# Strassen's seven products for the strided query and key tiles of a hybrid decoder trunk

## The chip, the cores and the metric

The kernel runs on one core of a Trainium2 chip. The metric is the device time of one execution in microseconds. Engines are named as in the profile: PE (TensorE, matrix products; PEld is its weight load), DVE (VectorE), ACT (ScalarE), POOL (GpSimd, which here mostly issues DMAs) and SP (SyncE, which issues DMAs). Each engine takes its instructions in the order in which the program wrote them; an instruction that waits holds back all that stand behind it on the same engine.

## The reference

A two-layer decoder trunk on x of 512 tokens by 1024 features. Layer 0 mixes tokens with dilated window attention, layer 1 with a gated linear recurrence; each is followed by a gated FFN with a short causal convolution, and each part is wrapped in a norm before and a norm after. The change touches layer 0's attention alone:

```
WINDOWS, DILATIONS = (128, 512, 2048), (1, 4, 16)
qkv = (x @ w_qkv).reshape(B, S, N_GROUPS, 3, HEADS_PER_GROUP, HEAD_DIM)   # 3 groups of 8 heads of 128
for g in range(N_GROUPS):
    o, lse = dilated_group_attention(qkv[:, :, g, 0], qkv[:, :, g, 1], qkv[:, :, g, 2], ...)
alpha = jax.nn.softmax(jnp.stack(lses), axis=0)
o = jnp.sum(alpha[..., None] * jnp.stack(outs), axis=0)
return o.reshape(B, S, ATTN_OUT_WIDTH) @ w_o
```

Group 0 (dilation 1) is called local here, groups 1 and 2 strided. Both strided groups are computed together, with the tokens permuted by their residue mod 4.

## The kernel before

**Split weights.** Every large product is done in three passes over float32r parts: both operands are split into a high part (a rounded copy, made by ScalarE, line 144) and a low part (the difference, made by VectorE, line 145), and high x high, high x low, low x high are summed in PSUM (`mm3`, L325). So a tile of 128 features by 512 tokens over 1024 rows is 8 x 3 = 24 matmuls of 512 columns.

**The supply of weights.** `plan` lists all weight chunks in order, one raw chunk of 1 MB each, loaded by SP (`load`, L267) into three raw buffers. `refill` turns a chunk into pieces, in order; `pump` takes the next piece, if one of the 16 weight buffers (`HALVES`, counted in `state["live"]`) is free, and splits it. `take` hands a piece to the matmuls, `done` gives its buffers back. `tick` is called after each tile: it lets the side tasks go on (`side`: softmax work written as generators, which yield how many ticks to wait) and then pumps one or two pieces.

**The attention, as it stands.** Per pair of heads (`hp`), four pairs. The local stage computes values, queries and keys of group 0 with 24-matmul tiles, with `local` as a side task for each head. Then come four strided rounds, each of eight query and key tiles (`feat_tiles(4, ...)`, L325, for two groups), four value blocks of 24 matmuls (`values`, L1028), and two heads as side tasks (`strided`). A head multiplies queries and keys (S, L1124), adds the bias and takes the maximum (VectorE), exponentiates (ScalarE), normalises, transposes in VectorE, stores the result to DRAM (`turned`, L368), fetches it back transposed (`fetched`, eight DMAs, L375) and broadcasts a row of factors (`cn`, L1160); all these DMAs are issued by POOL. Some ticks later it multiplies by the values (O, L1179). The value blocks go through DRAM to be permuted (SP, L1040 and L1053). `qk` (L941, L943) scales a finished tile out of PSUM, permuting it. After the rounds, `rows_run` multiplies by `w_o` and applies the norms.

**Strassen in the FFN.** `seven` already does this for eight chunks of the FFN's upward product. A chunk of 1024 rows by 256 features is seen as 2 x 2 blocks, and so is the token operand: four products of one block of features, rows and tokens for each half of the result, eight in all, become seven products of sums of blocks, each 4 x 3 matmuls of 256 columns (L830). The token side's sums are made once per layer (`token_sums`): 8 passes to add the parts, 8 to combine, 8 splits. They take the buffer of x (`x_sb`), which is saved to DRAM and fetched back by `x_back`, and one or two gain buffers. The weight side's sums are made in the raw chunk, some by VectorE (L195, L199), some by a DMA issued on POOL that adds a block from DRAM into the raw tile (`add_rows`, L181). `slot` emits one product or one filling quarter, then what `later` put off, then a tick.

**Order.** The program order is fixed by hand; there is no scheduler that moves instructions.

Of the kernel before, what the change touches and what calls it, by code (L numbers as in the profile page):

```python
# [11 lines left out]
F32 = mybir.dt.float32  # L12
# [6 lines left out]
P = 128  # L19
# [21 lines left out]
CYCLE = 15  # L41
HALF = ("s1", "w11", "w12", "a22", "s2", "s3", "s4")
# [36 lines left out]
def kernel(  # L79
# [136 lines left out]

    def refill():

        i = state["cv"]
        if i >= state["dma"]:  # L220
            return
# [13 lines left out]
    def pump(limit=2):  # L235

        for _ in range(limit):
# [4 lines left out]
            if pieces and state["live"] + 2 - (pieces[0][0][1] in HALF) <= HALVES:  # L242
# [47 lines left out]
    def tick():  # L290
        for s in list(sides):
            s[0] -= 1
# [436 lines left out]
    def token_sums(hT, T):  # L729

        assert len(sides) == 1
        d = dp.tile([P, 4, D], F32, name=nm("x_kept"))
        nc.gpsimd.dma_start(d, X[0])
        kept.append(d)
        homes = cp.tile([P, 4, D], F32R, tag="x_sb", name=nm("T"))
        homes = [homes[:, n] for n in range(4)]
        homes += [cp.tile([P, D], F32R, tag="gain", name=nm("T"), bufs=2) for _ in range(2)]
        homes = [[h[:, 0:512], h[:, 512:1024]] for h in homes]
        homes += [[gen(F32R, "T") for _ in range(2)] for _ in range(2)]
# [9 lines left out]
        tt = nc.vector.tensor_tensor  # L749

# [14 lines left out]
        for k in range(2):  # L765
            tt(b12[k], b12[k], b22[k], op=ALU.subtract)
            tt(b22[k], b22[k], b11[k], op=ALU.add)
# [3 lines left out]
        yield 8  # L771
        parted(2, b12)
        yield 3
        b21 = whole(4, 0)
        yield 1
        for k in range(2):
            tt(b21[k], b21[k], b22[k], op=ALU.subtract)
# [5 lines left out]
    def seven(hT, T, begin, before):  # L783

        due = []

        def later(n, f):
            due.append([n, f])

        def slot(emit):  # L790
            emit()
            for d in list(due):
                d[0] -= 1
                if d[0] < 0:
                    due.remove(d)
                    d[1]()
            tick()
# [7 lines left out]
        right = {  # L805
            1: block(0, 0), 2: block(1, 0), 3: block(1, 1), 5: turn(0), 6: turn(1), 7: turn(2), 4: turn(3),
        }

# [45 lines left out]
        def quarters(i, m, j, b):  # L854
            ps = []

            def quarter(n):
                W = take(i, m)
                if not n:
                    ps.append(psum())  # L860
                for k in (2 * n, 2 * n + 1):
                    mm3(
                        ps[0], [w[k // 4][:, k % 4, :] for w in W], [h[:, k, :] for h in hT], k == 0, k == KD - 1
                    )
                if n % 2:
                    done(1)
                if n == 3:
                    later(1, lambda: finish(b, ps[0], j))

            return [lambda n=n: quarter(n) for n in range(4)]  # L870

        steps = {}
        fill = quarters(before, 1, SEVEN[0] - 1, 3)
        for n, j in enumerate(SEVEN):
# [3 lines left out]
            steps.update((CYCLE * n + m, q) for m, q in zip((1, 2, 6, 7, 10, 11, 12, 13), fill + quarters(i, 0, j, 2)))  # L878
            fill = quarters(i, 1, j, 3)
# [4 lines left out]
        fill += quarters(after, 0, SEVEN[-1] + 1, 0)  # L884
# [10 lines left out]
    def attention(hT, post, pre):  # L895
# [119 lines left out]
        def values(vs, permute, midway=None):  # L1015

            if permute:
                vd = dp.tile([S, 512], F32, name=f"vrows{len(vrows)}")
                vrows.append(vd)
            ids = [chunk(), chunk()]  # L1020
            banks = {}
            for t in range(4):
                banks[t] = psum("v")
                for u in range(4):
                    W = take(ids[u // 2], u % 2)
                    steps = [(k, a, b) for k in (2 * u, 2 * u + 1) for a, b in PASSES]
                    for k, a, b in steps:
                        mm(  # L1028
                            banks[t],
# [404 lines left out]
```

## Time and profile before

| | |
|---|---|
| median of 3 runs | 1443.12 us (1443.1 to 1443.16) |
| profiled execution | 1443.5 us |
| its span | 1441.7 us |
| busy PE / DVE / ACT / POOL | 1433.2 / 924.9 / 674.7 / 179.5 us |
| granted TensorE clock | 0.999 |

The profile's page gives busy times of each engine, a picture of the span in 40 slices, DMA queues, the chain of work that ended last, and the costliest groups of instructions. A row of a group names the line, engine, operation, out<-in tiles, shapes and count, then total busy time and mean nanoseconds of one, then the idle time before them and what ended it. A row of the timeline has the start, the length, the engine, line, operation and, in brackets, the idle time before it with the engine or DMA that ended it. A row of the stage windows has start:end, then the length, then busy time (and number of instructions) of PE, PEld, DVE, ACT and POOL, the granted clock, the share of the DMA engines and GB/s. Busy times count an instruction from its start to its end; back to back they overlap a little.

### The profile page before, as it was taken

What the parts mean: (1) busy time and instruction counts of PE and PEld (TensorE: products, weight loads), DVE (VectorE), ACT (ScalarE), POOL (GpSimd) and SP (SyncE); (2) the same over time, 40 slices, a digit from 0 to 9 for tenths busy, and PEclk for the clock granted to TensorE, in tenths of its full rate; (3) what the DMA queues carried; (4) which work ended last, traced back from release to release, by engine and by line L of the source; (5) the groups of instructions that cost most, each with busy time, mean ns of one, the idle gap of its engine ahead of it and who ended that gap; (6) DMA issues with size and microseconds to landing.
All of it is one profiled execution on the core that took longest, in us unless ns stands there. A gap on an engine that the chain in (4) does not pass through costs nothing.

```text
span 1441.7 us, 20040 instructions
## 1 busy us (share of the span) xinstructions
PE 1433.2 (99%) x7437; PEld 1229.6 (85%) x7437; DVE 924.9 (64%) x1851; ACT 674.7 (47%) x1380; POOL 179.5 (12%) x311
## 2 busy tenths in 40 slices
PE   9999999999999999999999999999999999999998
PEld 7888888888888898989988888888898899988886
DVE  6555635353536889877774348869789977774333
ACT  7333424141415555555543335589455555553331
POOL 0441514040402101101000001000100111000000
PEclk9999999999999999999999999999999999999999
DMA  7653546364636345554452322431435645453201
GB/s 224 206 150 108 170 119 187 127 182 132 182 133 191 117 147 122 145 133 104 142 205 88 108 82 88 132 117 59 146 98 155 150 107 128 126 189 117 88 0 59
DMA packets 142842, 189.63 MB, mean 132 GB/s; under 512 B 9312, under 2 KB 119352, under 8 KB 142232
## 3 DMA queue, kind: packets, MB, share of 16 engines
q1 hardware_dynamic: 114280, 145.48, 31.6%
q0 software_dynamic: 27616, 41.82, 12.4%
q8 instruction: 58, 0.95, 0.3%
q10 hardware_dynamic: 848, 1.05, 0.2%
q14 instruction: 40, 0.33, 0.1%
HBM read 168.83 MB, written 19.49 MB: 131 GB/s over the span
## 4 chain that ended last, share of the span: by engine, by line
PE 92%; ACT 4%; DVE 3%; issue 0%; DMA 0%; DVEq 0%; ACTq 0%
PE ps L325 44%; PE acc L325 24%; PE ps L830 11%; PE v L1028 8%; PE v L956 1%; DVE xb L1237 1%; PE O L1179 1%; PE S L1124 1%; PE S L1078 1%; DVE wlo L145 1%; ACT sig L1258 1%; ACT whi L144 1%; PE O L325 1%; PE tr L407 1%; ACT sig L1277 0%
## 5 line engine op out<-in xcount | busy, mean ns | idle before, releaser
L325 PE MATMUL ps<-hT,whi 128*128 128x512 f32 (+1 forms) x2240 | 644.9, 373 | 0.0
L144 ACT ACTIVATE whi<-raw 128x512 fp32r<-128x512 f32 x552 | 326.1, 626 | 322.6 <-PE ps L325 122.2
L145 DVE TENSOR_TENSOR wlo<-raw,whi 128x512 fp32r<-128x512 f32 x552 | 360.8, 686 | 180.1 <-ACT whi L144 180.1
L325 PEld LDWEIGHTS ps<-hT,whi 128*128 128x128 f32 x2240 | 403.9, 189 | 68.4
L325 PE MATMUL ps<-hT,wlo 128*128 128x512 f32 (+1 forms) x1120 | 415.7, 371 | 0.0
L325 PEld LDWEIGHTS ps<-hT,wlo 128*128 128x128 f32 x1120 | 211.0, 188 | 37.2
L325 PE MATMUL acc<-whi,ahi 128*128 128x512 f32 x512 | 199.6, 390 | 0.0
L325 PE MATMUL acc<-whi,alo 128*128 128x512 f32 x512 | 199.3, 389 | 0.1
L325 PE MATMUL acc<-wlo,ahi 128*128 128x512 f32 x512 | 199.2, 389 | 0.0
L678 DVE SCALAR_TENSOR_TENSOR u<-ps,cols,u 128x511 f32<-128x511 f32 x192 | 143.7, 748 | 48.9 <-ACT u L674 45.5
L325 PEld LDWEIGHTS acc<-whi,alo 128*128 128x128 f32 x512 | 96.1, 188 | 20.5 <-DVE alo L145 0.5
L325 PEld LDWEIGHTS acc<-wlo,ahi 128*128 128x128 f32 x512 | 96.1, 188 | 19.8
L325 PEld LDWEIGHTS acc<-whi,ahi 128*128 128x128 f32 x512 | 96.1, 188 | 19.7
L674 ACT ACTIVATE u<-ps,cols 128x512 f32<-128x512 f32 x96 | 74.0, 770 | 82.3 <-DVE ps L845 41.9
L1028 PE MATMUL v<-whi,hT 128*128 128x512 f32 x320 | 102.3, 393 | 0.0
L830 PE MATMUL ps<-T,whi 128*128 128x256 f32 x512 | 92.8, 280 | 0.0
L181 POOL DMA_DIRECT2D raw<-in_ffn_w_up_dram x32 | 41.5, 1475 | 362.0 <-DVE wlo L145 207.8
L368 POOL DMA_DIRECT2D turned<-T x36 | 19.6, 547 | 523.7 <-DVE T L362 522.4
L375 POOL DMA_DIRECT2D ft<-turned x144 | 78.8, 555 | 43.4 <-issue 18.1
L830 PEld LDWEIGHTS ps<-T,whi 128*128 128x128 f32 x512 | 80.1, 189 | 1.6
L830 PE MATMUL ps<-T,wlo 128*128 128x256 f32 x256 | 71.8, 280 | 0.0
L1028 PEld LDWEIGHTS v<-whi,hT 128*128 128x128 f32 x320 | 60.1, 188 | 12.2
(194 smaller groups left out, 1483.9 us busy)
## 6 DMA issues: line engine op xcount, KB each, us to landing
raw<-in_ffn_w_up_dram SPq DMA_DIRECT2D x48, 1024.0 KB
raw<-in_attn_w_qkv_dram SPq DMA_DIRECT2D x67, 512.0 KB
raw<-in_ffn_w_down_dram SPq DMA_DIRECT2D x24, 1024.0 KB
raw<-in_ffn_w_up_dram POOLq DMA_DIRECT2D x32, 256.0 KB, 4.6
raw<-in_lru_w_in_dram SPq DMA_DIRECT2D x8, 1024.0 KB
turned<-T POOLq DMA_DIRECT2D x28, 256.0 KB, 2.7
ft<-turned POOLq DMA_DIRECT2D x112, 64.0 KB, 5.5
vrows<-v SPq DMA_DIRECT2D x16, 256.0 KB
```

Source lines behind the costliest of these rows:

```text
L144: nc.scalar.activation(hi, raw, AF.Copy)
L145: nc.vector.tensor_tensor(lo, raw, hi.bitcast(F32), op=ALU.subtract)
L181: nc.gpsimd.dma_start(to, src, accum_op=ALU.add)
L325: mm(dst, l[a], r[b], start=start and n == 0, stop=stop and n == 2)
L368: nc.gpsimd.dma_start(d, T)
L375: nc.gpsimd.dma_start(t[32 * c : 32 * c + 32].rearrange("j (b x) -> j b x", b=4), d.rearrange("(b j) (c x) -> c j b x", j=32, c=4)[c],)
L407: nc.tensor.transpose(ps[:, k * P : (k + 1) * P], xs[i][:, k * P : (k + 1) * P], ident)
L674: nc.scalar.activation(u, ps, AF.Identity, scale=cc[:, j : j + 1], bias=cc[:, 48 + j : 49 + j])
L678: nc.vector.scalar_tensor_tensor(u[:, d:], ps[:, : S - d], wc, u[:, d:], op0=ALU.mult, op1=ALU.add)
L830: mm(y[b][:, 0:256], W[wa][0][:, k, :], right[n](ha, k), start=n in (1, 5) and k == q == 0, stop=k == 3 and q == 2, skip_group_check=True,)
L956: mm(banks[t], hT[a][:, k, t * P : (t + 1) * P], W[b][k % 2][:, 0, :], start=u == n == 0, stop=u == 3 and n == 5,)
L1028: mm(banks[t], hT[a][:, k, t * P : (t + 1) * P], W[b][k % 2][:, 0, :], start=(k, a, b) == (0, 0, 0), stop=(k, a, b) == (KD - 1, 1, 0),)
```

## The change

All 16 strided query and key chunks are computed as seven block products each (a chain), in place of 48 matmuls of 512 columns. A round of two heads is 44 slots of one product or one value quarter: four chains that start 7 slots apart (`APART`; the products of one at slots 0, 2, 3, 4, 6, 8, 12, `QUAD`), and the 16 value quarters (6 matmuls of 512 columns each) at slots 28, 30 to 32, 34 to 43, 45 and 49 (`QUARTERS`), the last two of them in the next round. A slot counts as a quarter of a tick for the side tasks, and splits at most one piece. The heads' tasks are cut into smaller steps and start two slots after the fourth chain's last product: the first head's S in slot 35 of the round, the second's in slot 39; their transposes and DMAs are emitted two slots after each S.

The weight side: of a chunk, three sums are made by VectorE in the raw tile (`first`, `second`, `fourth`) and one by an adding DMA on POOL (in `second`, read by the piece `s3`). Pieces are split in the order of `strided_stream`: w11, s1, w12, s2, s4 at 0, 2, 3, 4, 6 of a chain, s3 at 10.5, a22 at 12, the value pieces at 28, 30, 31, 32 of the round. A piece takes one of the 16 weight buffers, a value piece two.

The result side: ScalarE copies three partial sums out of PSUM (after products 1, 5, 6), VectorE adds two (after 3 and 7) and scales the halves (`qk`).

The token sums are made in the local stage, with some signs turned. They take the buffer of x (fetched again from the input in the last round), one gain buffer, two general buffers and two of the 16 weight buffers until the rounds end. The tables `rights`, the helper `quarters` and `slot`, `later` move out of `seven` and are shared. The last local tile is done in quarters in and before the first round, and the last two local heads run in its first slots.

```diff
+QUAD = {1: 0, 5: 2, 2: 3, 6: 4, 3: 6, 7: 8, 4: 12}
+APART, ROUND = 7, 44
+QUARTERS = (28, 30, 31, 32, 34, 35, 36, 37, 38, 39, 40, 41, 42, 43, 45, 49)
...
+    def strided_stream(i0):
+        items = []
+        for r in range(4):
+            for c in range(4):
+                i, o = i0 + 6 * r + c, ROUND * r + APART * c
+                def first(i=i):
+                    x = blocks(i)
+                    nc.vector.tensor_tensor(x["s1"], x["s1"], x["a22"], op=ALU.add)
+                def second(i=i):
+                    x = blocks(i)
+                    nc.vector.tensor_tensor(x["s1"], x["s1"], x["w11"], op=ALU.add)
+                    add_rows(x["w11"], plan[i][3][0][0][:, 0:4, P:256])
+                def fourth(i=i):
+                    x = blocks(i)
+                    nc.vector.tensor_tensor(x["w12"], x["w12"], x["s1"], op=ALU.add)
+                for at, item in (
+                    (0, ("w11", "w11")), (0.1, (None, first)), (2, ("s1", "s1")), (2.1, (None, second)),
+                    (3, ("w12", "w12")), (4, ("s2", "s1")), (4.1, (None, fourth)), (6, ("s4", "w12")),
+                    (10.5, ("s3", "w11")), (12, ("a22", "a22")),
+                ):
...
+            for u in range(4):
+                i = i0 + 6 * r + 4 + u // 2
...
+                items.append((ROUND * r + QUARTERS[u], ((i, u % 2), cuts, u % 2 == 1)))
+        return [item for _, item in sorted(items, key=lambda x: x[0])]
...
-            if pieces and state["live"] + 2 - (pieces[0][0][1] in HALF) <= HALVES:
+            if not pieces or pieces[0][0][0] >= state["dma"]:
+                continue
+            if state["live"] + 2 - (pieces[0][0][1] in HALF) <= HALVES:
...
-    def token_sums(hT, T):
+    def token_sums(hT, T, first=False):
+        if first:
+            x_src = x[0].rearrange("(t p) d -> p t d", p=P)
...
+            homes += [[gen(F32R, "T") for _ in range(2)]]
+            homes += [[wp.tile([P, 512], F32R, tag=t, name=nm("T")) for _ in range(2)] for t in ("hi", "lo")]
+            state["live"] += 2
...
+        def chain(right, out, scale):
+            i = chunk()
+            y, t = {}, []
+            def step(n):
+                W = take(i, LEFT[n][0])
+                b, at = {1: (1, 0), 6: (1, 0), 7: (1, 0), 4: (1, 0), 5: (0, 256), 3: (0, 256), 2: (0, 0)}[n]
+                if b not in y:
+                    y[b] = psum()
+                dst = y[b][:, at : at + 256]
+                for k in range(4):
+                    for q, (wa, ha) in enumerate(PASSES):
                         mm(
+                            dst, W[wa][0][:, k, :], right[n](ha, k), start=n in (1, 5) and k == q == 0,
+                            stop=k == 3 and q == 2, skip_group_check=True,
                         )
+                done(1)
+                if n == 1:
+                    t.extend(gen(s="part") for _ in range(2))
+                if n in (1, 5, 6):
+                    to = {1: t[0][:, 0:256], 6: t[0][:, 256:512], 5: t[1][:, 0:256]}[n]
+                    later(1, lambda: nc.scalar.activation(to, dst, AF.Copy))
+                elif n == 3:
+                    def upper():
+                        nc.vector.tensor_tensor(t[0], y[0], t[0], op=ALU.add)
+                        out[0] = qk(t[0], scale, True)
+                    later(1, upper)
+                elif n == 7:
+                    later(1, lambda: nc.vector.tensor_tensor(y[1][:, 256:512], dst, t[1][:, 0:256], op=ALU.add))
+                elif n == 4:
+                    def lower():
+                        out[1] = qk(y[1], -1.0 if scale is None else -scale, True)
+                    later(1, lower)
...
+            for c in range(4):
+                f = chain(right, pairs[c // 2][c % 2], None if c % 2 else SCALE)
+                steps.update((ROUND * hp + APART * c + QUAD[p], f(p)) for p in QUAD)
+            def heads(hp=hp, pairs=pairs, vs=vs):
+                for hh in range(2):
+                    side(strided(2 * hp + hh, hh, pairs, vs), 0.25 + hh)
+                if hp == 3:
+                    x_back()
+            end = ROUND * hp + max(QUAD.values()) + 3 * APART
+            steps[end] = lambda f=steps[end], g=heads: (f(), later(2, g))
+            steps.update((ROUND * hp + n, q) for n, q in zip(QUARTERS, value_quarters(vs, prep if hp == 3 else None)))
+        state["even"] = True
...
+        for n in range(max(steps) + 1):
+            if n in steps:
+                slot(steps[n], 0.25)
...
-            w_cols(qkv, g * 3 * D + j * D + hp * 256, True)
+            w_cols(qkv, g * 3 * D + j * D + hp * 256, True, "quad")
```

More of the change, by code (lines that the diff above doesn't have):

```diff
@@ L781, with rights @@
     LEFT = {5: ("s1", 1), 1: ("w11", 0), 3: ("s4", 1), 2: ("w12", 0), 6: ("s2", 1), 7: ("s3", 1), 4: ("a22", 1)}
[L783 to L797, printed above, removed]
+    def rights(hT, T):
         def block(kr, n):
@@ L883, in seven @@
         steps[end + 3] = steps.pop(max(steps))
-        fill += quarters(after, 0, SEVEN[-1] + 1, 0)
+        fill += fillers(after, 0, SEVEN[-1] + 1, 0)
         for m in range(max(steps) + 1):
```

230 lines of the change are left out of this document (151 added, 79 removed).

## The prediction

> **What bounds the kernel now.** I read the busy shares first, then the chain of work that ended last, then stage windows cut at the round boundaries that this chain shows.
>
> ```profile
> PE 1433.2 (99%) x7437; PEld 1229.6 (85%) x7437; DVE 924.9 (64%) x1851; ACT 674.7 (47%) x1380; POOL 179.5 (12%) x311
> ```
>
> ```profile
> 60.04:198.15 138.11, 138.11 (x663) 116.26 (x662) 79.85 (x214) 52.16 (x135) 50.53 (x92) 1.00 0.52 152
> 209.06:281.61 72.55, 72.55 (x354) 61.20 (x353) 34.52 (x94) 22.72 (x62) 15.25 (x28) 1.00 0.54 156
> 281.61:354.16 72.55, 72.55 (x354) 61.20 (x353) 34.51 (x94) 22.84 (x62) 15.22 (x28) 1.00 0.53 157
> 354.16:426.70 72.54, 72.54 (x353) 61.20 (x353) 34.51 (x94) 22.73 (x62) 15.23 (x28) 1.00 0.53 157
> ```
>
> TensorE is the bound: it has no idle time in three whole strided rounds of 72.55 us, at a granted clock of 1.00, while VectorE works 34.5 us of each, ScalarE 22.8 and POOL 15.2. Only fewer matmul columns or a new wait of TensorE can move the time. The chain gives the pieces (start, length, line, matmuls):
>
> ```profile
> 209.06 5.44 PE v L1028 x24
> 214.50 1.78 PE S L1124 x16
> ...
> 281.61 5.44 PE v L1028 x24
> 287.05 1.78 PE S L1124 x16
> 288.83 5.46 PE v L1028 x24
> 294.29 1.78 PE S L1124 x16
> 296.07 10.90 PE v L1028 x48
> 306.97 16.32 PE ps L325 x72
> 323.29 1.78 PE O L1179 x16
> ...
> 359.60 1.78 PE S L1124 x16
> ...
> 890.02 5.75 PE ps L325 x48
> ```
>
> A 512-column matmul takes 10.90/48 = 0.2271 us (the tiles the same: 16.32/72 = 0.2267); a 256-column one, in the long run at 890 us, 5.75/48 = 0.1198.
>
> **The change, term 1: TensorE's work.** A round computes eight query and key tiles, 8 x 24 x 0.2267 = 43.5 us. It becomes 4 chains of 7 products of 12 matmuls of 256 columns: 28 x 12 x 0.1198 = 28 x 1.437 = 40.25 us. The 16 value quarters (6 x 0.2271 = 1.363 us each, 21.8 us) and the two S and two O blocks (7.1 us) stay. A round falls from 72.55 to 69.2 us; four save 13.5.
>
> The Trainium skill (TensorE: Matmul & The Clock Gate, "Back-to-back issue gap") has an isolated spacing of N/2.4 + 2.5 ns: 109.2 ns at 256 columns, 215.8 at 512. By it, an estimate, a round would save 41.4 - 36.7 = 4.7 us and four 18.9; the trace has 119.8 and 227.1 ns, so it is not used.
>
> **Term 2: VectorE and ScalarE.** Each chain splits seven half tiles instead of four, adds three blocks in place, and combines partial sums.
>
> ```profile
> 29.15 4.90 DVE L145 TENSOR_TENSOR wlo<-raw,whi 128x512 fp32r<-128x512 f32 x8
> ```
>
> ```profile
> L144 ACT ACTIVATE whi<-raw 128x512 fp32r<-128x512 f32 x269 | 155.9, 625 | 144.5 <-PE ps L325 87.7 <-DMA raw<-in_attn_w_qkv_dram 32.5 <-PE ps L830 15.2
> L836 ACT ACTIVATE part<-ps 128x256 f32<-128x256 f32 x7 | 2.6, 367 | 0.0
> ```
>
> ```profile
> 50.00:100.00 50.00, 50.00 (x237) 41.84 (x236) 35.11 (x102) 19.47 (x49) 19.99 (x39) 1.00 0.64 194
> 550.00:600.00 50.00, 50.00 (x290) 44.19 (x289) 45.85 (x74) 27.81 (x50) 6.34 (x5) 1.00 0.53 118
> ```
>
> Back to back, a 512-wide VectorE pass takes 4.90/8 = 0.61 us. A round gains 12 splits, 12 block adds, 4 full and 4 half-width combines: 28 x 0.61 + 4 x 0.37 = 18.6, so 34.5 becomes 53.1 of 69.2 us (77%). ScalarE gains 12 x 0.625 + 12 x 0.367 = 11.9 and has 34.7 of 69.2. The FFN's Strassen stage carries VectorE at 45.85 of 50 with TensorE always busy, so the average is covered. Two places are tight. The token sums add 24 passes (14.6 us) to VectorE in about the stretch 50 to 100, where 35.1 + 14.6 nearly fills it. And the last two local heads now fall among the first chains. Between 0 (the splits run ahead) and 5 us (a few late local heads) I take 2. Rewriting x into SBUF (2 MB on POOL's queue, issued with the last heads) and the two gain loads on SP's queue, which now also wait for a token sum, have the four output chunks ahead of their first reader: 0, at most 2 if the load is late for the first post norm.
>
> **Term 3: the accumulating DMA.** This is where I expect the loss. Each chain's piece s3 is the sum of w11 and the upper right block, made by a DMA that adds the second into the first in the raw tile (add_rows). It is issued on POOL, whose queue runs in program order and also carries the softmax traffic of the heads. So I count slots. From slot 34 to 41 of a round only value quarters run. The 16 weight buffers then hold 2 token sums, 8 value halves and 6 pieces of the next round: five of its first chain and w11 of its second. The second chain's s1, and with it the add, waits for the first release, in slot 42. The two heads emit their transposes, fetches and row broadcasts in slots 37 and 41. Hence the second chain's add stands behind both heads in POOL's queue, in rounds 2, 3 and 4. POOL's rows for two heads (S at 287.05):
>
> ```profile
> 296.52 1.14 POOL L368 DMA_DIRECT2D turned<-T  x2 [46.60 <-DVE T L362]
> 297.65 0.54 POOL L1156 DMA_DIRECT2D crow<-s  x1
> 300.25 4.36 POOL L375 DMA_DIRECT2D ft<-turned  x8 [2.06 <-DMA turned<-T]
> 306.81 0.56 POOL L1160 DMA_DIRECT2D cn<-crow  x1 [2.20 <-DMA ft<-turned]
> 307.36 1.08 POOL L916 DMA_DIRECT2D toe<-rowv  x2
> 308.44 1.08 POOL L368 DMA_DIRECT2D turned<-T  x2
> 309.51 0.54 POOL L1156 DMA_DIRECT2D crow<-s  x1
> 313.88 4.36 POOL L375 DMA_DIRECT2D ft<-turned  x8 [3.83 <-DMA turned<-T]
> 321.05 0.56 POOL L1160 DMA_DIRECT2D cn<-crow  x1 [2.81 <-issue]
> ```
>
> ```profile
> 247.74 0.56 POOL L1160 DMA_DIRECT2D cn<-crow  x1 [2.50 <-DMA ft<-turned]
> ...
> 393.62 0.56 POOL L1160 DMA_DIRECT2D cn<-crow  x1 [3.38 <-DMA ft<-turned]
> ```
>
> ```profile
> L181 POOL DMA_DIRECT2D raw<-in_ffn_w_up_dram x16: 1274/1286/1853, 529.2 to 691.8; - x16
> ...
> DMA to landing us min/median/max: 4.4/4.7/5.8
> ```
>
> Both heads leave POOL 33.8, 34.6 and 34.6 us after the first S began (248.30 - 214.50, 321.61 - 287.05, 394.18 - 359.60). The second S follows the first after four value quarters, 7.24 us, before as after the change, so I keep 34.3. The add then lands 4.7 us after its issue, at +39.0.
>
> Who waits: the split of s3 reads this sum. One piece is split per slot from 42 on (second chain s1, w12; first chain s3; second s2; first a22; second s4; third chain w11, s1, w12), so s3 of the second chain is emitted in slot 51. From there ScalarE, in order too, stands. Queued behind it is the copy of the second chain's first product out of PSUM (slot 52), and its product 6 (slot 55) may not add into that bank before the copy. TensorE reaches slot 55 at 1.78 + 5.45 + 1.78 + 5.45 (S, four quarters, S, four quarters) + 8.47 (slots 44 to 49, four products and two quarters) + 7.19 (five products) = +30.1. The copy ends at 39.0 + 0.63 + 0.37 = +40.0. So TensorE stands 9.9 us in each of three rounds: 29.7.
>
> Bounds: POOL's issues alone, without the bracketed waits for landings, end at 9.5 + 14.2 = +23.7; the add lands at +28.4, the copy is done at +29.4, and nothing is lost. With the slowest landing, 5.8, it is 11 a round. The waits are in all three rounds, so I take the measured end. Other rounds' adds (first chain, before the heads; third and fourth, after the late one) are hidden.
>
> **Sum** against the profiled execution, 1443.5 us (span 1441.7; the median of the runs is 0.4 less): 1443.5 - 13.5 + 2 + 29.7 = 1461.7, or 1461 on the median. ScalarE and VectorE, held some 13 us, have backlog after each stall; the next deadlines have one to two slots each, so I add nothing.
>
> **The rivals.**
> 1. The adds arrive in time, and term 1 is left: 1443.1 - 13.5 = 1430. For it: about 11 of the 34 us on POOL are waits for landings. It decides if the copy is done by +30.1, the add issued by about +24.4, ten earlier than the rows say. Against: all three rounds agree within 0.8 us. Chance 0.25.
> 2. Half of the waits go, 4.4 us a round: 1443.1 - 13.5 + 2 + 13.2 = 1445. Chance 0.12.
> 3. VectorE becomes the bound instead. In slots without value quarters a chain asks 13 x 0.61 + 0.37 = 8.3 us of each 10.06; with the value splits of those slots (8 x 0.61 in 40 us) 95%, and two late heads push it over. Counted at 5 us a round with no POOL wait: 1450. The FFN at 92% speaks against; it is inside rival 2 and my range, 0.03.
> 4. POOL's issues stretch as VectorE gets busier. The adds' 1274 to 1853 ns is a spread of 45%; on 14.2 us of issue that is 6.4 more a round: 1480. The median, 1286, is near the minimum, so 0.04. The Trainium skill (SBUF - State Buffer, "SBUF: two separate sides") says that POOL cannot write a DMA's descriptors while VectorE holds the shared port; by that rule, the trace hardly agrees, in the stage with VectorE at 45.85 of 50.
>
> **How the numbers follow.** My forecast has 0.56: 1461, own range 1450 to 1468. A measurement tells about 0.2%, 2.9 us, from no change. Faster (under 1440.2) is rival 1 and a little of rival 2: 0.27. Within 0.2% is the middle of rival 2: 0.06. The rest, 0.67, is slower. The range 1430 to 1469 leaves out the lower half of rival 1 and rival 4 with the top of the forecast.
>
> **What will show it.** Term 1: a product of 12 matmuls in 1.43 us and 69 us of TensorE work a round. Term 3: three waits of about 13 us of ScalarE's split for the raw tile's DMA, each just after two heads on POOL; POOL's issue of the accumulating DMA right behind the second broadcast (cn<-crow); TensorE idle some 10 us before a product in rounds 2 to 4 and none there in round 1. Wrong: TensorE without such gaps and rounds of 69 us (rival 1), or gaps whose releaser is VectorE (rival 3).

## The result and the profile after

The changed kernel takes 1492.57 us (median of four runs, 1492.01 to 1493.65) against 1443.14 before: 1.034 times the time, 95% interval 1.0325 to 1.0361. The prediction said slower, 1461 us with a range of 1430 to 1469. The time is 31.6 us above the forecast and outside the range.

The page of the kernel after: first the engines' busy time, then the granted TensorE clock in 40 slices of the span.

```profile
PE 1433.5 (96%) x8013; PEld 1255.9 (84%) x8013; DVE 1019.2 (68%) x2003; ACT 719.9 (48%) x1484; POOL 198.8 (13%) x328
...
PEclk9999999898989899999999999999999999999999
```

TensorE is busy as long as before (1433.2 us), but the span has grown by 48.5, from 1441.7 to 1490.2 us. So it now stands still 56.7 us, where it stood 8.5. And four slices of the clock are an 8, three in rounds 2 to 4 and one at the end of the last; before, all forty were a 9.

The stage windows of the kernel after (start:end, length, busy PE, PEld, DVE, ACT, POOL, clock, DMA share, GB/s). They are cut at the S of local head 5 (heads are counted from 0), the last S ahead of the last local tiles, and then at the first S of each of the four rounds; so the first row holds the end of the local stage and round 1 up to its first S:

```profile
144.50:221.80 77.30, 71.13 (x490) 66.46 (x488) 58.58 (x122) 36.35 (x87) 30.56 (x50) 0.98 0.57 151
221.80:305.10 83.30, 71.92 (x498) 67.78 (x496) 54.89 (x126) 33.10 (x86) 20.26 (x32) 0.92 0.55 149
305.10:387.40 82.30, 71.63 (x498) 67.49 (x496) 54.87 (x126) 33.01 (x86) 20.29 (x32) 0.92 0.55 151
387.40:469.10 81.70, 71.83 (x498) 67.63 (x497) 52.65 (x122) 32.93 (x86) 19.81 (x32) 0.94 0.62 187
```

From one round's first S to the next it was 72.55 us. It is now 83.3, 82.3 and 81.7, with about 10.6 us of standing still in each. The timeline of TensorE has every wait between 146 and 514 us that is longer than 0.95 us (start, length, instruction; in brackets the wait before it and what ended it):

```profile
178.69 0.51 PE L1151 MATMUL ps<-T,whi 128*128 128x256 f32 x2 [1.70 <-DVE ps L1169]
188.49 0.50 PE L1151 MATMUL ps<-T,whi 128*128 128x256 f32 x2 [0.97 <-ACT part L1160]
193.66 0.50 PE L1151 MATMUL ps<-T,whi 128*128 128x256 f32 x2 [3.50 <-DVE ps L1169]
263.44 0.79 PE L1151 MATMUL ps<-T,whi 128*128 128x256 f32 x2 [11.38 <-ACT part L1160]
346.03 0.80 PE L1151 MATMUL ps<-T,whi 128*128 128x256 f32 x2 [10.67 <-ACT part L1160]
427.54 0.80 PE L1151 MATMUL ps<-T,whi 128*128 128x256 f32 x2 [9.87 <-ACT part L1160]
...
506.50 4.47 PE L1315 MATMUL O<-ft,vp 128*128 128x128 f32 x16 [7.92 <-DMA vp<-vrows]
```

There are three places: round 1 (6.2 us), slot 55 of rounds 2 to 4 (31.9 us), and the end of the last round (7.92 and three short ones, 10.0 us).

**Slot 55.** POOL's queue and ScalarE, around the first of the three long waits:

```profile
247.10 4.38 POOL L439 DMA_DIRECT2D ft<-turned  x8 [3.39 <-ACT part L1160]
253.89 0.57 POOL L1296 DMA_DIRECT2D cn<-crow  x1 [2.41 <-DMA ft<-turned]
254.64 2.53 POOL L184 DMA_DIRECT2D raw<-in_attn_w_qkv_dram  x2 [0.18 <-DMA vrows<-v]
```

```profile
262.49 0.63 ACT L147 ACTIVATE whi<-raw 128x512 fp32r<-128x512 f32 x1 [12.57 <-DMA raw<-in_attn_w_qkv_dram]
263.03 0.37 ACT L1160 ACTIVATE part<-ps 128x256 f32<-128x256 f32 x1
```

The second head's broadcast leaves POOL, and right behind it come two adding DMAs, those of the second and the third chain. ScalarE stands 12.57 us at the split of s3, then copies the partial sum, and TensorE goes on as that copy ends, at 263.44. The group of the adding DMAs in the rounds (L184, 200 to 440 us) says who waited for them (ScalarE's splits, 35.5 us in three waits) and how long they took to land:

```profile
  ACT whi L147: 35.5, 3
...
DMA to landing us min/median/max: 4.1/6.0/9.4
```

**The clock.** Windows around the same wait (the clock is the third number from the end):

```profile
255.00:263.00 8.00, 0.00 (x0) 0.00 (x0) 0.00 (x0) 0.51 (x1) 2.16 (x2) 0.54 0.97 215
263.50:265.50 2.00, 2.00 (x9) 2.00 (x10) 1.90 (x5) 1.43 (x4) 0.00 (x0) 0.50 0.15 18
...
267.50:269.50 2.00, 2.00 (x12) 2.00 (x12) 1.21 (x3) 1.43 (x3) 0.00 (x0) 0.53 0.86 253
269.50:272.00 2.50, 2.50 (x23) 2.50 (x22) 2.46 (x5) 0.24 (x1) 1.19 (x1) 1.00 0.71 209
```

After the wait TensorE runs at half clock for 5.9 us. The first pair of matmuls takes 0.79 us there and 0.50 after the waits of 1.70 and 0.97 us. After the wait of 3.50 us in round 1 it takes 0.50 too, but there the half clock follows 0.6 us later (two windows of the kernel after):

```profile
190.88:194.29 3.41, 0.63 (x5) 0.64 (x6) 3.41 (x7) 0.18 (x1) 0.11 (x1) 1.00 0.83 127
194.29:197.70 3.41, 3.41 (x18) 3.41 (x18) 0.50 (x1) 0.00 (x0) 1.34 (x3) 0.50 1.06 380
```

The Trainium skill (TensorE: Matmul & The Clock Gate, "What's actually happening") gives the rule: the clock halves after an idle window of about 3.4 us, comes back after a busy one of the same length, and these windows are free-running: they do not reset when a kernel starts. The trace agrees with the halving, and with a return that takes longer than one window: TensorE was back at 263.44, the full clock at 269.35. The last section shows that here the window need not be idle as a whole.

**The end.** SP's queue and ScalarE at the end of the last round of the kernel after:

```profile
494.62 1.68 SPq L1130 DMA_DIRECT2D vrows<-v  x1
503.34 1.76 SPq L1183 DMA_DIRECT2D vp<-vrows  x4
```

```profile
489.22 4.27 ACT L147 ACTIVATE whi<-raw 128x512 fp32r<-128x512 f32 x8
493.39 0.68 ACT L1129 ACTIVATE v<-v,first_y 128x512 f32<-128x512 f32 x1
```

The last value product ends at 486.48. ScalarE evicts its block 6.9 us later, behind eight splits of FFN weights. It is stored at 494.62, behind two loads of weight chunks that SP issued at 491.78 and 494.19, and only 8.7 us later can the four permuted loads go out, for which O waits. In the kernel before, the last value product ends at 452.07 and its eviction follows at once; the loads go out 3.7 us after the store (452.82 and 456.56), and O begins without a wait. ScalarE's row and the chain of the kernel before:

```profile
452.10 0.69 ACT L1039 ACTIVATE v<-v,first_y 128x512 f32<-128x512 f32 x1 [1.44 <-PE v L1028]
```

```profile
463.85 3.57 PE O L1179 x32
```

**The local stage.** Windows of the kernel before, then of the kernel after:

```profile
60.00:146.00 86.00, 86.00 (x411) 72.14 (x409) 50.40 (x143) 32.50 (x83) 25.90 (x48) 1.00 0.48 143
```

```profile
60.00:146.00 86.00, 86.00 (x410) 72.10 (x409) 61.76 (x160) 37.08 (x91) 27.35 (x49) 1.00 0.45 134
```

VectorE works 11.4 us more in this stretch, with the token sums in it, and TensorE is full in both: they cost nothing.

### The profile page after: what moved, and what is told of

It is laid out like the page before. It is cut to its first block, busy times and chain, and to the rows that moved or that the text cites. A ratio compares the mean times of both kernels' runs of the same rounds, so it can differ in the third digit from the quotient of the medians.

```text
span 1490.2 us, 21561 instructions
## 1 busy us (share of the span) xinstructions
PE 1433.5 (96%) x8013; PEld 1255.9 (84%) x8013; DVE 1019.2 (68%) x2003; ACT 719.9 (48%) x1484; POOL 198.8 (13%) x328
## 4 chain that ended last, share of the span: by engine, by line
PE 80%; DVE 7%; ACT 6%; DMA 4%; issue 2%; POOL 0%; DVEq 0%; ACTq 0%; POOLq 0%; SPq 0%
PE ps L389 30%; PE acc L389 23%; PE ps L918 11%; PE ps L1151 7%; PE v L1091 4%; DMA raw<-in_attn_w_qkv_dram 2%; DVE wlo L148 2%; ACT L L1274 1%; PE v L1029 1%; ACT whi L147 1%; DVE xb L1408 1%; PE O L1315 1%; DMA ft<-turned 1%; DVE L L1196 1%; ACT sig L1429 1%
## 5 line engine op out<-in xcount | busy, mean ns | idle before, releaser
L148 DVE TENSOR_TENSOR wlo<-raw,whi 128x512 fp32r<-128x512 f32 x600 | 395.6, 687 | 247.5 <-ACT whi L147 246.9
L147 ACT ACTIVATE whi<-raw 128x512 fp32r<-128x512 f32 x600 | 356.0, 627 | 333.0 <-PE acc L389 118.2
L389 PE MATMUL ps<-hT,whi 128*128 128x512 f32 (+1 forms) x1728 | 486.0, 367 | 0.0
L389 PEld LDWEIGHTS ps<-hT,whi 128*128 128x128 f32 x1728 | 308.2, 189 | 48.9
L389 PE MATMUL ps<-hT,wlo 128*128 128x512 f32 (+1 forms) x864 | 316.0, 366 | 0.0
L389 PEld LDWEIGHTS ps<-hT,wlo 128*128 128x128 f32 x864 | 162.9, 189 | 26.9
L1151 PE MATMUL ps<-T,whi 128*128 128x256 f32 x512 | 101.6, 297 | 38.1 <-ACT part L1160 32.9
L1151 PEld LDWEIGHTS ps<-T,whi 128*128 128x128 f32 x512 | 85.6, 203 | 40.5 <-ACT part L1160 33.7
L1091 PE MATMUL v<-whi,hT 128*128 128x512 f32 x320 | 107.1, 397 | 0.0
L918 PE MATMUL ps<-T,whi 128*128 128x256 f32 x512 | 92.8, 280 | 0.0
L184 POOL DMA_DIRECT2D raw<-in_ffn_w_up_dram x32 | 41.5, 1464 | 362.8 <-DVE wlo L148 226.9
L439 POOL DMA_DIRECT2D ft<-turned x144 | 79.1, 557 | 40.6 <-DMA turned<-T 11.2
L918 PEld LDWEIGHTS ps<-T,whi 128*128 128x128 f32 x512 | 80.1, 189 | 1.6
```

Source lines behind the costliest of these rows:

```text
L147: nc.scalar.activation(hi, raw, AF.Copy)
L148: nc.vector.tensor_tensor(lo, raw, hi.bitcast(F32), op=ALU.subtract)
L184: nc.gpsimd.dma_start(to, src, accum_op=ALU.add)
L389: mm(dst, l[a], r[b], start=start and n == 0, stop=stop and n == 2)
L439: nc.gpsimd.dma_start(t[32 * c : 32 * c + 32].rearrange("j (b x) -> j b x", b=4), d.rearrange("(b j) (c x) -> c j b x", j=32, c=4)[c],)
L918: mm(y[b][:, 0:256], W[wa][0][:, k, :], right[n](ha, k), start=n in (1, 5) and k == q == 0, stop=k == 3 and q == 2, skip_group_check=True,)
```

## The experiments

The ratio is always to the kernel before on the same chip, with its 95% interval. For each kernel the table has the start of the S of local head 5, then the time from there to the first S of round 1, from that to the first S of round 2, and so on, and from the first S of round 4 to the end of the span (all from the timeline of TensorE, us). So slot 55, the twelfth slot of round 2, stands in the column of round 2.

| kernel | to S of head 5 | round 1 | round 2 | round 3 | round 4 | rest |
|---|---|---|---|---|---|---|
| before | 144.6 | 69.8 | 72.6 | 72.6 | 72.5 | 1009.7 |
| after | 144.5 | 77.3 | 83.3 | 82.3 | 81.7 | 1021.1 |
| e1 early add | 144.3 | 77.0 | 71.9 | 71.9 | 72.5 | 1021.4 |
| e2 no add | 144.6 | 74.8 | 70.6 | 70.7 | 71.0 | 1021.6 |
| e3 end | 144.4 | 77.8 | 84.5 | 82.0 | 81.5 | 1009.4 |
| e4 filled waits | 145.2 | 76.7 | 81.3 | 81.1 | 81.6 | 1020.9 |
| e5 = e1 + e3 | 145.1 | 77.4 | 73.3 | 72.6 | 70.7 | 1008.4 |
| e6 = e5 + held splits | 144.6 | 75.0 | 72.3 | 73.1 | 74.0 | 1008.3 |
| e7 = e6 + lows on POOL | 145.3 | 82.4 | 73.9 | 71.3 | 70.4 | 1014.7 |
| e8 = e6 + later s3 | 145.0 | 74.8 | 72.5 | 70.8 | 71.8 | 1012.0 |
| e9 = e8 + some lows on POOL | 144.4 | 75.4 | 77.0 | 75.0 | 71.6 | 1008.4 |
| e10 = e8 + head 7 later | 145.3 | 74.3 | 72.1 | 72.1 | 71.1 | 1010.5 |
| e11 = e10 + last head earlier | 145.4 | 75.4 | 71.6 | 71.5 | 72.2 | 1012.9 |
| e12 = e11 + two more holds | 145.9 | 73.3 | 71.6 | 70.7 | 71.8 | 1010.2 |

**e1: the second chain's add ahead of the heads.** Its w11, s1 and with them the adding DMA are split and issued before POOL gets the heads' DMAs.

```diff
+                    if r and c == 1 and at < 2.5:
+                        at = -3.5 + at / 10
                     items.append((o + at, item))
```

> In rounds 2 to 4 the pieces w11 and s1 of the second chain are split three pieces earlier, so that their adding DMA is issued before the two heads' DMAs on POOL; nothing else moves. Theory (the late add on POOL holds ScalarE, and the copies behind it hold product 6): the three waits before slot 55 (11.4, 10.7 and 9.9 us of TensorE idle) go, and with them the slow matmuls behind each (some 2.6 us each): 1492.6 - 32 - 8 = 1453. Rival (VectorE or the chunk loads are late anyway, and the stall only moves to another slot): 1475 or more, with idle of TensorE in the same rounds released by VectorE or by a load.

Measured: 1464.93 us (1460.8 to 1467.29), ratio 1.0148 (1.0129 to 1.0166). Windows of rounds 2 and 4:

```profile
221.30:293.20 71.90, 69.83 (x497) 65.14 (x496) 54.76 (x126) 32.64 (x86) 20.19 (x32) 1.00 0.63 173
...
365.10:437.60 72.50, 69.82 (x497) 65.29 (x497) 51.62 (x121) 32.84 (x86) 18.57 (x31) 1.00 0.65 198
```

The three long waits are gone and the clock is full: rounds 2 to 4 lose 31.0 us of length (table), and the median of the time falls by 27.6 us; the profiled execution is the fastest of the four. The place in POOL's queue is the cause. The theory's 1453 is not reached: these rounds still hold 6.6 us of short waits, and the slow matmuls were worth about 2 us a round, not 2.6. Round 1 and the end, which it left alone, keep their waits (77.0 and 1021.4 us).

**e2: no adding DMA at all.** s3 lacks the block that the DMA adds; TensorE's work is the same.

```diff
                     nc.vector.tensor_tensor(x["s1"], x["s1"], x["w11"], op=ALU.add)
-                    add_rows(x["w11"], plan[i][3][0][0][:, 0:4, P:256])
```

> The adding DMA is left out of all 16 chains (so the piece s3 lacks a block and the strided keys and queries are not the reference's); every other instruction stays. Theory of the late add: no wait of ScalarE for the raw tile's adding DMA, no stall at slot 55 in any round: 1450 to 1453, and the first round's idle (6.2 us) stays, since VectorE makes it. Rival: 1475 or more. If it lies well under the run with the early add, the other adds cost something too.

Measured: 1455.09 us (1454.93 to 1456.38), ratio 1.0085 (1.0069 to 1.0102). TensorE's timeline, the waits of rounds 2 to 4:

```profile
252.34 0.50 PE L1150 MATMUL ps<-T,whi 128*128 128x256 f32 x2 [1.29 <-DVE ps L1168]
323.00 0.50 PE L1150 MATMUL ps<-T,whi 128*128 128x256 f32 x2 [1.35 <-DVE ps L1168]
394.02 0.50 PE L1150 MATMUL ps<-T,whi 128*128 128x256 f32 x2 [1.38 <-DVE ps L1168]
```

All adds together cost 37.5 us, 9.8 more than e1 regained: the adds that e1 leaves cost something too. Even with none the kernel is slower than before: what is left are one short wait for VectorE in each round, round 1 and the end.

**e3: the end alone.** The last value block is evicted one slot sooner, and the splits of FFN weights wait until it is out.

```diff
-                    later(1, lambda: evict(t))
+                    later(0 if prep and t == 3 else 1, lambda: evict(t))
...
+                state["hold"] = n >= 174
                 slot(steps[n], 0.25)
```

> Only the end of the last round is changed: the last value block is evicted in the slot of its last quarter, and no piece is split from slot 174 on until the output product begins. Theory (the values' way through DRAM ends last there: ScalarE's eviction stands behind eight splits, and the store lands late beside weight loads): the 7.9 us wait of O for the fetched values goes, with some 2 us of slow matmuls: 1492.6 - 10 = 1483. Rival (the heads' own DMAs end last): O then waits for the broadcast row instead, and at most 3 us go: 1489.

Measured: 1481.56 us (1481.24 to 1485.1), ratio 1.0271 (1.0256 to 1.0287), 11.0 us less than the kernel after. O's wait falls from 7.92 to 0.84 us, and the rest after the rounds is 1009.4 us long, as before the change. Counted from round 4's first S, the eviction comes 4.2 us sooner (490.33 - 470.21 against 493.39 - 469.09), and from the store to the permuted loads it is 4.8 us (491.02 to 495.78) instead of 8.7, since the held splits hold back the weight loads too (SP issues the next ones from 498.51 on). So the splits ahead of the eviction were the cause; what part of it was ScalarE's order and what the loads beside the store, e3 does not separate.

**e4: the half clock.** While TensorE waits in slot 55, it runs 42 matmuls of 512 columns into a bank that nobody reads; their sum, 42 x 0.227 = 9.5 us, fits into the wait.

```diff
+            if n in (54, 98, 142):
+                idle = psum("idle")
+                for _ in range(42):
+                    mm(idle, hT[0][:, 0, 0:P], hT[0][:, 0, :], start=True, stop=True)
```

> After slots 54, 98 and 142, where TensorE stands still, 42 matmuls of 512 columns (9.5 us) are added whose result nobody reads. Theory (an idle stretch of some 10 us lowers the granted clock, and the matmuls behind it run at about half speed for some us): the same stalls filled with useless work make the kernel faster by about 3 x 2.6 = 8 us: 1485. Without that: 1492 to 1494, no change. If the stall were not of the length of a fixed wait but moved with the work, it would be slower by up to 28 us.

Measured: 1489.95 us (1486.01 to 1492.71), ratio 1.0322 (1.0303 to 1.0341). The same place:

```profile
263.38 0.50 PE L1151 MATMUL ps<-T,whi 128*128 128x256 f32 x2 [1.62 <-ACT part L1160]
265.57 0.51 PE L1151 MATMUL ps<-T,whi 128*128 128x256 f32 x2 [0.53 <-DVE ps L1169]
```

The product now starts at full clock at the same moment (263.38 against 263.44), but 2.2 us later there is a wait for VectorE that was not there. The rounds lose 2.0, 1.2 and 0.1 us in the profiled execution: removing the half clock alone regains 3.3 of about 6 us there. The median falls by 2.6 us, and the runs spread over 6.7, so the size is not firm. The new wait speaks for a backlog of ScalarE and VectorE, from their own standing still, that lies partly beside the half clock; no run tests that by itself.

**e5, e6: both repairs, then round 1.** e5 is e1 and e3 in one kernel. e6 adds that in five slots of round 1 no piece is split.

```diff
-                state["hold"] = n >= 174
+                state["hold"] = n >= 174 or n in (10, 12, 14, 15, 16)
```

> Both single edits in one kernel: the second chain's sum, copy and adding transfer ahead of the heads, and the last value block evicted at once with the splits behind it held. Theory (the two losses stand in different rounds and share no work): the gains add. The early add took 27.6 us off the changed kernel's 1492.6 and the end's edit 11.0 us, so 1492.6 - 27.6 - 11.0 = 1454 us, with the wait of product O for vp under 2 us and no wait of 10 us at slot 55. Rival (with the rounds faster, ScalarE and the loads reach the end later and the hold only moves the wait): 1460 us or more, with a wait of several us at the output product or at the first slots behind it.

> As the kernel with both edits, and in slots 10, 12, 14, 15 and 16 of round 1 no piece of the coming weights is split, while heads 6 and 7 of the local stage still occupy VectorE. Theory (round 1's waits of 1.7, 1.0 and 3.5 us are VectorE saturated by two heads and the splits at once): those 6.2 us of waits shrink to under 2 and the slow matmuls behind them go, so 5 to 7 us below the kernel without this edit, 1446 to 1449 us. Rival (the held splits are missed some slots later, at the round's second half): the waits move behind slot 16 and the time stays within 2 us.

Measured: e5 1451.51 us (1449.05 to 1457.22), ratio 1.0063 (1.0043 to 1.0084); e6 1449.42 us (1448.85 to 1449.82), ratio 1.0044 (1.0027 to 1.006). The two gains add, to within e5's spread: 1453.9 would be their sum. e6's hold shortens round 1 by 2.4 us, less than half of what was expected, and rounds 3 and 4 give some back. Its waits in rounds 2 to 4 that ScalarE ended:

```profile
262.28 0.51 PE L1153 MATMUL ps<-T,whi 128*128 128x256 f32 x2 [1.58 <-ACT part L1162]
...
335.40 0.50 PE L1153 MATMUL ps<-T,whi 128*128 128x256 f32 x2 [2.40 <-ACT part L1162]
...
408.35 0.50 PE L1153 MATMUL ps<-T,whi 128*128 128x256 f32 x2 [2.18 <-ACT part L1162]
```

and before the second of them, on POOL and on ScalarE:

```profile
325.14 0.56 POOL L1298 DMA_DIRECT2D cn<-crow  x1 [3.53 <-DMA ft<-turned]
325.75 1.25 POOL L184 DMA_DIRECT2D raw<-in_attn_w_qkv_dram  x1
```

```profile
334.45 0.63 ACT L147 ACTIVATE whi<-raw 128x512 fp32r<-128x512 f32 x1 [6.68 <-DMA raw<-in_attn_w_qkv_dram]
```

The third chain's add, too, stands behind the heads, and takes 8.7 us from issue to use. It was hidden behind the second's as long as that one was late.

**e7, e9: low parts on GpSimd.** In e7 GpSimd makes the low parts of all value pieces of the rounds, in e9 (on top of e8) those of rounds 2 and 3 alone. The code shown is e7's.

```diff
-    def split(hi, lo, raw):
+    def split(hi, lo, raw, low=None):
         nc.scalar.activation(hi, raw, AF.Copy)
-        nc.vector.tensor_tensor(lo, raw, hi.bitcast(F32), op=ALU.subtract)
+        (low or nc.vector).tensor_tensor(lo, raw, hi.bitcast(F32), op=ALU.subtract)
...
-                    split(hi, lo, raw)
+                    split(hi, lo, raw, nc.gpsimd if state["even"] and plan[key[0]][0] == "value" else None)
```

> As the kernel before it in this list, and the low parts of the strided value pieces are made by GpSimd, which takes 8 subtractions of 0.61 us a round, 4.9 us, off VectorE. Theory (the small waits left in rounds 2 to 4, about 2 us a round, are VectorE's backlog): they go, 4 to 7 us over the rounds, 1440 to 1445 us. Rival (the subtractions on GpSimd take longer, and GpSimd and VectorE delay each other, or the transfers that GpSimd issues stand behind them): the waits change their releaser to POOL or to a transfer and the time is 1448 us or more.

> As the kernel before it in this list, and GpSimd makes the low parts of the value pieces of rounds 2 and 3 alone. With these subtractions on GpSimd in every round, rounds 3 and 4 took 71.3 and 70.4 us from first S to first S, against 73.1 and 74.0 without, while round 1 and the end lost more than that. Theory (VectorE's backlog costs 1 to 3 us in each of these rounds): 2 to 5 us below the kernel before it, 1438 to 1443 us. Rival (what shortened those rounds was their later start against the loads, not VectorE's relief): within 1 us of the kernel before it or slower.

Measured: e7 1458.67 us (1456.61 to 1463.79), ratio 1.0113 (1.0093 to 1.0133); e9 1452.65 us (1449.07 to 1453.76), ratio 1.0055 (1.0039 to 1.0072). The theory fell. The group of these instructions in e7:

```profile
L148 POOL TENSOR_TENSOR wlo<-raw,whi 128x512 fp32r<-128x512 f32 x32 | 45.2, 1443 | 22.5 <-ACT whi L147 22.5
```

and two waits of TensorE, in e7 and in e9:

```profile
214.84 0.58 PE L391 MATMUL O<-plo,vhi 128*128 128x256 f32 x1 [4.10 <-DVE plo L1237]
```

```profile
291.01 0.50 PE L1157 MATMUL ps<-T,whi 128*128 128x256 f32 x2 [2.24 <-DVE ps L1175]
```

One takes 1443 ns, and POOL waits 22.5 us for ScalarE's high parts in between, with the heads' DMAs and the adds behind it on its queue. e9 makes exactly the rounds longer that it meant to relieve (77.0 and 75.0 us, against 72.5 and 70.8 in e8); so that e7's rounds 3 and 4 were short can't be put down to VectorE's relief.

**e8: the third chain's s3 later.** It is split 3.5 pieces later, with a22 ahead of it.

```diff
+                    if r and c == 2 and at > 10:
+                        at = 14 if item[0][1] == "s3" else 10.5
...
-                        item = ((i, item[0]), lambda i=i, h=item[1]: [blocks(i)[h]], item[0] == "a22")
+                        item = ((i, item[0]), lambda i=i, h=item[1]: [blocks(i)[h]], item[0] == ("s3" if r and c == 2 else "a22"))
```

> As the kernel with the early add, the end's edit and the held splits (1449.4 us); in rounds 2 to 4 the third chain's s3 is split 3.5 pieces later, behind two more pieces, with a22 ahead of it. Theory (what is left of the transfers' cost is the third chain's add: behind the heads on GpSimd's queue it lands at 261.3, 334.4 and 407.4 us, ScalarE stands 6.7 us on it in round 3 with other splits behind it, and TensorE waits 1.58, 2.40 and 2.18 us for the copy of a product): these three waits go, 5 to 6 us, 1443 to 1445 us. Rival (VectorE and ScalarE are the bound in these slots, the transfer only the last releaser): the waits come back as waits for VectorE, and the time stays at 1447 us or more.

Measured: 1446.94 us (1443.88 to 1452.51), ratio 1.0027 (1.0013 to 1.004). No wait of rounds 2 to 4 is ended by ScalarE any more, and these rounds take 4.3 us less than e6's. The rest takes 3.7 more:

```profile
468.55 0.71 PE L1319 MATMUL O<-ft,vp 128*128 128x128 f32 x4 [2.03 <-DMA vp<-vrows]
470.07 0.71 PE L1319 MATMUL O<-ft,vp 128*128 128x128 f32 x4 [0.81 <-DMA vp<-vrows]
```

The mechanism is confirmed; most of its gain went back into the same wait of O that e3 had removed.

**e10, e11, e12: what is left of round 1 and of the end.** e10 lets head 7 (the second of the two local heads in round 1) start two slots later; e11 lets the last strided head start two slots earlier; e12 holds the splits in slots 7 and 8 too.

```diff
-                side(local(6 + hh, hh, q, k, v), 0.5 + hh)
+                side(local(6 + hh, hh, q, k, v), 0.5 + 1.5 * hh)
```

```diff
-                    side(strided(2 * hp + hh, hh, pairs, vs), 0.25 + hh)
+                    side(strided(2 * hp + hh, hh, pairs, vs), 0.25 + (hh / 2 if hp == 3 else hh))
...
-                state["hold"] = n >= 174 or n in (10, 12, 14, 15, 16)
+                state["hold"] = n >= 174 or n in (7, 8, 10, 12, 14, 15, 16)
```

> As the first kernel of this list, and the second of the two local heads that run in round 1 starts two slots later. Theory (round 1's remaining waits of 1.63, 1.51, 0.69 and 1.18 us come from both heads' VectorE work falling together): at least half of them go, 2 to 3 us below the first kernel of this list. Rival (they come from VectorE's sum of work over the stage, not from its bunching): the waits move by some slots and the time stays within 1 us.

> As the kernel with the later second local head (1446.9 us); in the last round alone the second strided head starts two slots earlier, so that ScalarE's exponentials of that head (451.25 to 454.24 us) are over when the last value block is complete at 452.0. Theory (at the end the eviction of the last value block stands behind those exponentials: vp arrives late and product O waits 1.69 us in the middle): the wait goes, 2 to 4 us, 1443 to 1445 us. Rival (the store and the loads of vp land late because of other transfers, whenever they are issued): the wait stays above 1 us and the time within 1 us of 1446.9.

> As the kernel before it in this list, and in slots 7 and 8 of round 1 too no piece is split. Theory (the wait of 3.41 us at 179.69 comes about because the last operation of product 7 stands on VectorE behind the low part of a piece whose high part stands on ScalarE behind a local head's exponentials; in order, one behind the other): the wait goes, 3 us, 1440 to 1442 us, under the kernel before the change. Rival (the exponentials themselves hold the evictions): the wait stays above 2 us.

Measured: e10 1446.9 us (1443.57 to 1448.68), ratio 1.0021 (1.0011 to 1.003); e11 1449.2 us (1445.41 to 1450.79), ratio 1.0037 (1.0024 to 1.0049); e12 1447.26 us (1444.83 to 1448.58), ratio 1.0024 (1.0015 to 1.0033). e10's rival held: four waits of round 1 (4.9 us in e8) became two of 3.41 and 1.43. In e11 O no longer waits for vp, but the transposes of the last head now wait for VectorE:

```profile
456.25 1.94 PE L1310 MATMUL PT<-ident,L 128*128 128x128 f32 x8 [2.76 <-DVE L L1291]
```

where they waited 0.90 us in e10. The wait changed places, and the time did not fall. e12's theory held for the place, not for the time: the 3.12 us that e11 still waited there became 0.91, and the next wait, for the same copy by ScalarE, grew from 1.60 to 2.15. The page of e12 and its waits in round 1:

```profile
PE 1422.0 (99%) x8013; PEld 1244.8 (86%) x8013; DVE 1018.7 (71%) x2003; ACT 717.8 (50%) x1484; POOL 199.6 (14%) x330
```

```profile
179.22 0.50 PE L1155 MATMUL ps<-hT,whi 128*128 128x256 f32 x2 [0.91 <-ACT part L1164]
200.26 0.51 PE L1155 MATMUL ps<-T,whi 128*128 128x256 f32 x2 [2.15 <-ACT part L1164]
```

e12 has the whole saving in TensorE's work, 1433.2 - 1422.0 = 11.2 us, and a span of 1443.6 us, 1.9 above the kernel before: 13.1 us more of standing still use it up. No version beat the kernel before. These kernels also scatter (e8 over 8.6 us, the kernel before on the same chip over 0.6); the cause of that stays open.

## Why the prediction was right in direction and wrong in size

The sum on record was -13.5 + 2 + 29.7 = +18.2 us. In the same terms the span's +48.5 is: TensorE's work -11.2 (from e12), slot 55 +31.9, round 1 +6.2, the end +10.0, and 1433.5 - 1422.0 = 11.5 us of matmuls at reduced clock. (In the trace of the kernel after TensorE is busy for 25.4 us at half clock, so at most 12.7 us could be lost there.)

**Term 1 (-13.5): right mechanism, 2.3 us too large.** The table's step from 72.55 to 69.2 us a round is 69.8 us by e1's busy column, so 2.75 saved instead of 3.35. The hand count of 28 products and 16 quarters has nothing for the restart after each short wait (a pair of 0.50 us instead of 0.40): e2's rounds, with one such wait each, have 69.3, 69.3 and 69.6 us of work. The remainder of the 0.6 was not followed further.

**Term 2, the engines' work and the token sums: right.** A round has 54.9 us of VectorE's work and 33.1 of ScalarE's, where 53.1 and 34.7 were forecast (the half-width combine, put at 0.37 us from a row of ScalarE, takes VectorE 0.43), and the local stage ends at the same moment.

**Term 2, the last two local heads (0 to 5, taken 2): mis-sized.** They made 6.2 us of waits, all of them on VectorE or on a copy by ScalarE. The row of the FFN at 45.85 of 50 showed that an average of 92% can be hidden. It did not show what happens when softmax steps and splits stand in the same few slots: there a product's last addition comes behind a low part, which comes behind a high part, which comes behind exponentials (e12, where holding two splits took 3.12 us down to 0.91). Moving the two heads apart moved the waits and left their sum (e10).

**The end ("0, at most 2 if the load is late for the first post norm"): the step that failed outright.** I looked at the loads of x and the gains, which did cost nothing. What came late was the value block of the last round. Its products end as long before O is due as in the kernel before (12.1 us against 11.8), but ScalarE evicts it behind eight splits, and its store stands beside the weight loads that these splits made room for: 10.0 us of waits, 11.0 us of the time by e3.

**Term 3 (29.7): right in place, mechanism and size.** TensorE came to slot 55 at +30.3 us (263.44 - 11.38 - 221.80; forecast +30.1). The second broadcast left POOL at +32.7 (forecast 34.3) and the add followed it. The add landed 7.8 us after its issue and 6.1 in the two later rounds instead of 4.7, and the waits were 31.9 us. The earlier issue and the longer landing partly cancel, so that the size fits within 2.2 us is in part luck. The waits are there in full in all three rounds, so rival 1 (the adds in time) and rival 2 (half) are out, and e1 takes them away by an earlier place in POOL's queue. "Other rounds' adds ... are hidden" was true only while the second chain's was late: e6 shows the third chain's, 6.2 us in three rounds, e8 removes it.

**"I add nothing" for the time after each wait: failed.** A TensorE that has stood 10 us comes back at half clock; 2.0 us a round by the windows (71.8 busy against e1's 69.8), of which e4's trace regains 3.3 in three rounds. With the half clock after the wait of 3.50 us in round 1 and after O's wait it is the 11.5 us above, a term that the sum had at nothing.

**Rival 3 (VectorE the bound, 5 us a round, 0.03)** is what is left when the rest is mended: with no adds at all e2 waits 1.3 us a round for VectorE, e8 1.2 to 2.7. It is real, a quarter to a half of the price, and hidden as long as the transfers are late. **Rival 4 (POOL's issues stretch)** is out: the eight fetches of a head take POOL 4.38 us in the kernel after, where they took 4.36 in the kernel before, and the adding DMAs' issues of rounds 2 to 4 stay at 1192 to 1255 ns in e6, with VectorE at 55 of 72 us.

So the range failed by three costs beside term 3: the end, the clock and round 1, together 27.7 us, for which the sum had 2.

## What to carry to other kernels

When a change saves work on the engine that bounds the kernel, and the order of all queues is fixed by hand, go through every in-order queue that feeds that engine, at the start and at the end of the changed stage as well as in its steady part; each of the three places here (slot 55, the end, round 1) was an instruction standing behind work that had nothing to do with it. A wait found is not the only one: when the second chain's transfer was mended, the third's came out, and behind it VectorE, until the 11 us saved were used up. A long wait of TensorE costs more than its length, because of the clock, but the surplus is worth less than it looks where the other engines have backlog anyway.

## What the runs showed of the hardware

The granted clock changes only at the borders of steps of 3.41 us: the half-clock stretches of the kernel after, up to O, are one, four, four, three and three steps long. How busy TensorE is within a step decides on the next step. In the fourteen traces, from 20 us on, each of the 37 full-clock steps in which it was busy for at most 0.42 of the step was followed by half clock, and of the 5802 busier ones only two were (0.51 and 0.55 of the step, both in e7). Half clock ended after each of the 25 steps with at least 0.83 busy and after none of the 32 with at most 0.80. So where a wait falls counts beside its length. A wait of 2.18 us within one step halves the clock in e6, the first two rows; one of 3.41 us that is spread over two steps does not in e10, the other two, nor in the step after them:

```profile
406.16:409.58 3.42, 1.24 (x11) 1.24 (x11) 1.43 (x3) 2.19 (x5) 0.00 (x0) 1.00 1.21 284
409.58:412.99 3.41, 3.41 (x18) 3.41 (x17) 3.29 (x6) 1.91 (x5) 0.00 (x0) 0.50 0.33 68
```

```profile
174.53:177.94 3.41, 1.75 (x15) 1.55 (x14) 1.54 (x9) 2.46 (x10) 0.00 (x0) 1.00 0.78 269
177.94:181.35 3.41, 1.66 (x14) 1.66 (x15) 3.35 (x8) 2.53 (x7) 0.28 (x1) 1.00 0.00 0
```

The same adding DMA of 256 KB that lands 4.7 us after its issue in the FFN takes 4.1 to 9.4 us, 6.0 in the median, in the attention rounds. A 512-wide subtraction takes GpSimd 1443 ns, where VectorE does it in 0.61 us back to back.
